# An encoder block on one core: four PSUM banks per tile in the first feed-forward product, a norm factor moved into the residual, SiLU as one function, and the last product's weights prepared in another stage

## The chip, the core and the metric

The kernel runs on one core of one Trainium2 chip. A core has five engines with a queue each: TensorE (PE, with its weight loads as PEld), VectorE (DVE), ScalarE (ACT), GpSimd (POOL) and SyncE (SP), which here issues all transfers. Each engine takes its instructions strictly in order; an instruction that waits for a semaphore holds up everything behind it on the same engine. The metric is the device time of one execution in microseconds, as the median of several runs. Times in this document are microseconds unless marked ns.

## The reference

Two sequences of 512 tokens with 1024 features go through one layer: a norm, a wide input projection, three branches (a state-space scan, a differential attention, a cross attention with a memory of 256 tokens), a gated merge, and a feed-forward part, then a final norm. The change touches the feed-forward part and the final norm:

```python
def _rmsnorm(x, g):
    y = xf * lax.rsqrt(jnp.mean(xf * xf, axis=-1, keepdims=True) + EPS)
    return (y * g.astype(jnp.float32)).astype(x.dtype)
...
    x = x + merged @ p['w_out'][l]
    xn2 = _rmsnorm(x, p['norm_ffn'][l])
    gate, up = jnp.split(xn2 @ p['w_ffn_in'][l], 2, axis=-1)
    return x + (jax.nn.silu(gate) * up) @ p['w_ffn_out'][l]
...
    return _rmsnorm(x, p['norm_final'])
```

The feed-forward width is 2816, which is 22 tiles of 128 columns. All arithmetic is fp32: each product is made of three TensorE products of a high and a low part (hh, hl, lh), so every fp32 weight or activation is first split, the high part by ACT (`L128`, or `L131` with a scale) and the low part by DVE (`L129`, or `L132` with a scale).

## The kernel before

The program is written as one function, `encoder`, and a scheduler fixes the order of each engine's queue when the program is built; where `PE.on` is true, TensorE keeps the order of the text. The stages, in time, are: memory and input projections with the state-space scan, cross attention, differential attention, merge, output projection (`out_tile`), first feed-forward product (called FFN-in here), second feed-forward product (FFN-out) and the final norm.

**Cross attention** (`L637` to `L685`) runs 32 steps of score, softmax, turn and output. Products from other stages are taken from a list (`queue`) and laid between the steps, so that TensorE has work while a softmax is made. Into the same steps goes `half_piece` (`L447`): one half of a *piece* of weights for FFN-out. There are 34 such pieces, made by the generator `prepare` (`L416`): two loads of `raw` from `w_fo` (`L402`, `L404`), four sums of 128x128 on POOL (`raw_sums`, `L411` to `L414`), a split into `hl` on ACT and DVE (`L131`, `L132`, with the scale 0.5), and a store to DRAM (`wD<-hl`, `L431`). FFN-out loads them later as `w<-wD`.

**FFN-in** (`L1069` to `L1098`) is a loop over 22 tiles. Both halves of a tile, gate and up, and both sequences together form a 2x2 block product, and it is made with seven products instead of eight (a Strassen-Winograd scheme). The seven have names: A11, S2, A12, S3, S1, A22 and S4. Each is 12 matmuls of 128x512 into a PSUM bank of its own, so a tile is 84 matmuls, and six banks rotate. The weights of a tile come as two loads (`wf<-in_w_fg` and `wf<-in_w_fu`, `L950` and `L951`); A11, A12 and A22 are splits of these, S1 to S4 are splits of four sums that POOL makes (`L965` to `L968`). `quadrants` (`L1049`) turns the seven banks into four quadrants with one ACT copy and seven DVE additions (`L1046`). Then, for each of the two sequences, the tile is finished so:

```python
            V.tensor_tensor(out=gf, in0=gf, in1=accs[s], op=ALU.mult)                                   # L1093
            last_t = S.activation(out=ac[:, cs], in_=gf, func=AF.Tanh, scale=0.5)                       # L1094
            PO.tensor_tensor(out=up, in0=up, in1=accs[s], op=ALU.mult)                                  # L1095
            V.scalar_tensor_tensor(out=ac[:, cs], in0=ac[:, cs], scalar=1.0, in1=gf, op0=ALU.add, op1=ALU.mult)  # L1096
            V.tensor_tensor(out=ac[:, cs], in0=ac[:, cs], in1=up, op=ALU.mult)                          # L1097
```

`accs[s]` holds the norm factor of each token; it is made while tile 0 is on TensorE (`L1087`, `L1088`). The result goes to DRAM (`aD`, `L1098`), twice too large (1 + tanh in place of a sigmoid), which the 0.5 in the splits of FFN-out's weights makes good.

**FFN-out** (`L1147` to `L1200`) takes the activations back from `aD`, sums and splits them (`act_pair`, `quad_split`), multiplies with the prepared and the freshly made weights, and adds to the residual `y`, which was stored to DRAM as `x1D` and is loaded again. The final norm (`final`, `L1214`) sums the squares of `y`, takes the root (`factor`, `L189`), spreads it over the partitions with TensorE transposes, and scales.

Of the kernel before, what the change touches and what calls it, by code (L numbers as in the profile page):

```python
# [19 lines left out]
P = 128  # L20
# [47 lines left out]
def encoder(ctx: ExitStack, tc: tile.TileContext, a, out):  # L68
# [112 lines left out]
    def rstd(acc, n, nt=4):  # L181


        ss = aux()
        for t in range(nt):
            PE.matmul(ss[:, t : t + 1], acc[:, t * P : (t + 1) * P], onec[:, 0:1], start=(t == 0), stop=(t == nt - 1))
        return factor(ss, n, nt)

    def factor(ss, n, nt=4, bias=epsc):  # L189

        rs = rp.tile([P, 4], F32, tag="rs", name="rs", bufs=4)
        S.activation(out=rs[:, :nt], in_=ss[:, :nt], func=AF.Sqrt, scale=1.0 / n, bias=bias)
        V.reciprocal(rs[:, :nt], rs[:, :nt])
        bc = aux()
        for t in range(nt):
            PE.transpose(bc[:, t * P : (t + 1) * P], rs[:, t : t + 1].broadcast_to([P, P]), ident)
        return rs, bc
# [218 lines left out]
    def prepare(es_):  # L416
        pq = es_.enter_context(tc.tile_pool(name="pq", bufs=1, side="right", reuse_waits="tile"))
        todo_, raws = [x_ for x_ in pieces if x_[2]], []

        def load():  # L420
            if len(raws) < len(todo_):
                raws.append(pq.tile([P, 4, P], F32, tag="raw", name="raw", bufs=4))
# [10 lines left out]
        for _ in range(3):  # L433
# [12 lines left out]

    def half_piece(behind_=()):  # L447
        with ExitStack() as es_:
            for i_ in behind_:
                es_.enter_context(tc.issue_after(i_.ins))  # L450
            return next(prep, None)
# [100 lines left out]

    pes = ExitStack()
    prep = prepare(pes)
    next(prep)


# [83 lines left out]
    for i in range(-AHEAD, len(steps) + 1):  # L641
# [41 lines left out]
    assert next(prep, None) is None  # L683
    pes.close()
# [320 lines left out]
    def product(ps, w, o, ks=range(4)):  # L1005
        wh, wl = w
        for k in ks:
            th, tl = ops[k]
            ws_ = slice(k * P, (k + 1) * P)
            PE.matmul(ps, wh[:, ws_], th[:, o], start=(k == 0), stop=False)  # L1010
            PE.matmul(ps, wh[:, ws_], tl[:, o], start=False, stop=False)
            PE.matmul(ps, wl[:, ws_], th[:, o], start=False, stop=(k == 3))
# [3 lines left out]
    def products(i, w):  # L1016
# [12 lines left out]
        elif i == KFF - 1:  # L1029
# [5 lines left out]
        else:  # L1035
            for nm, o in SEVEN:
                p_ = bank()
                product(p_, w[nm], o)
                yield p_
# [8 lines left out]

    def quadrants(ps, p0, other=("up", "gf")):  # L1049

        p1 = ap2.tile([P, L], F32, tag="p1", name="p1")
        S.copy(p1, p0)
# [8 lines left out]

    def act_pair(p, tag="ts"):
# [4 lines left out]
        return xa_, xb_, quad_sums(xa_, xb_, tag)  # L1067

    for i in range(KFF):  # L1069
        w = res0  # L1070
        if i > 0:
# [3 lines left out]
            next(wg)  # L1075
        if i == KFF - 3:
            open_tags(ses, side="right", ts=1)
# [5 lines left out]
        ps = products(i, w)  # L1083
        p0 = next(ps)
        if i == 0:
            for s in range(NS):
                _, bc = rstd(accs[s], DM)  # L1087
                S.copy(accs[s], bc)  # L1088
        gf0, gf1, up0, up1 = quadrants(ps, p0)
        ac = ap2.tile([P, NT], F32, tag="ac", name="ac")  # L1090
        for s, gf, up in ((0, gf0, up0), (1, gf1, up1)):
            cs = slice(s * L, (s + 1) * L)
            V.tensor_tensor(out=gf, in0=gf, in1=accs[s], op=ALU.mult)  # L1093
            last_t = S.activation(out=ac[:, cs], in_=gf, func=AF.Tanh, scale=0.5)  # L1094
            PO.tensor_tensor(out=up, in0=up, in1=accs[s], op=ALU.mult)  # L1095
            V.scalar_tensor_tensor(out=ac[:, cs], in0=ac[:, cs], scalar=1.0, in1=gf, op0=ALU.add, op1=ALU.mult)  # L1096
            V.tensor_tensor(out=ac[:, cs], in0=ac[:, cs], in1=up, op=ALU.mult)  # L1097
        nc.sync.dma_start(aD[i], ac)  # L1098

# [21 lines left out]
    def weights7(m, p, n):  # L1121
# [12 lines left out]
        if n < 7:  # L1134
            split(wa[:, :, 0], wa[:, :, 1], raw[:, 1:4], scale=0.5)
        if n == 0:
            raw_sums(raw)
            yield
            split(ws_[:, :, 0], ws_[:, :, 1], raw, scale=0.5)
# [12 lines left out]
    for v, (m, lo_, hi_) in enumerate(VISITS):  # L1152
# [34 lines left out]
        if v == 8:  # L1187
# [5 lines left out]
            for i in range(2 * NPAIR, KFF):  # L1193
# [3 lines left out]
                split(th, tl, ac, scale=0.5)  # L1197
# [4 lines left out]

    def ones(ss, sq, n, start=False, stop=False):

        for t in range(n // P):
            PE.matmul(ss[:, t : t + 1], sq[:, t * P : (t + 1) * P], onec[:, 0:1], start=(start and t == 0),
                      stop=(stop and t == n // P - 1))
# [6 lines left out]
    def final(ss, c0, n):  # L1214

        cs = slice(c0, c0 + n)
        _, bc = factor(ss, DM, n // P)
# [438 lines left out]
```

## Time and profile before

| | |
|---|---|
| median of 3 runs | 1651.76 us (1650.51 to 1655.25) |
| span of the profiled execution | 1652.8 us |
| PE / DVE / ACT / POOL busy in it | 97% / 70% / 39% / 33% |
| share of the chain of work that ended last | PE 69%, DVE 14%, DMA 6%, issue 5%, POOL 3%, ACT 2% |

The page gives the execution from its first to its last instruction (the span); it has no entry for time outside it, and the span stands 1.0 us above the median of the runs. "Busy" of a TensorE row includes waiting inside its pipeline, since ends of matmuls are modelled. In the windows view a line is one stretch of time: its length, then for PE, PEld, DVE, ACT and POOL the busy time with the number of instructions, the granted TensorE clock as a share of full speed, the DMA share and the GB/s. In the groups view a line is a set of equal instructions: engine, operation, out<-in, count, then busy time and the mean ns of one, then the idle time of the engine just before them and who ended it.

### The profile page before, as it was taken

To read this page: it belongs to the slowest core of one execution; us is meant where nothing else is said; L and a number is where in the kernel's file an instruction comes from. 1 tells how busy PE (TensorE), PEld (TensorE's weight loads), DVE (VectorE), ACT (ScalarE), POOL (GpSimd) and SP (SyncE) were. 2 spreads that over 40 slices of the span, in tenths; PEclk is the share of its full clock that TensorE was granted. 3 is DMA by queue.
4 is the path that set the end of the run, shared out by engine and by line. 5 is a ranking of instruction groups with operands and counts; after the bars stand their busy time and mean duration, and the time that the engine had idled before them with its cause. 6 is when DMAs were issued, how large, how long until landed. Compare 5 with 4: busy or idle time off the path is not lost.

```text
span 1652.8 us, 21658 instructions
## 1 busy us (share of the span) xinstructions
PE 1599.8 (97%) x7812; PEld 1316.8 (80%) x7812; DVE 1162.2 (70%) x1860; ACT 637.6 (39%) x1130; POOL 542.7 (33%) x444
## 2 busy tenths in 40 slices
PE   7999999899998999999999989999999999999997
PEld 5788788788887778877878878778888888778887
DVE  7957997155776666767365657888777777998655
ACT  6544323245554355565123442222223223242222
POOL 0001100001576222200243345565555553434352
PEclk9999999999999999999999999999999999999998
DMA  9354343737887111135453432322222222776522
GB/s 365 122 167 151 110 153 115 227 124 258 274 286 248 52 45 33 45 141 169 144 191 125 149 96 77 102 90 93 87 77 89 77 89 99 255 268 191 182 71 102
DMA packets 108202, 237.05 MB, mean 143 GB/s; under 512 B 13888, under 2 KB 50496, under 8 KB 108096
## 3 DMA queue, kind: packets, MB, share of 16 engines
q1 hardware_dynamic: 108096, 235.69, 42.8%
q8 instruction: 61, 1.00, 0.3%
q14 instruction: 45, 0.37, 0.1%
HBM read 166.73 MB, written 68.91 MB: 143 GB/s over the span
## 4 chain that ended last, share of the span: by engine, by line
PE 69%; DVE 14%; DMA 6%; issue 5%; POOL 3%; ACT 2%; SPq 1%; DVEq 0%; ACTq 0%; POOLq 0%
PE bkmm L61 60%; PE bktr L61 2%; DVE tl L129 2%; PE bksc L61 2%; DVE wl L129 2%; PE bkoo L61 1%; DMA raw<-in_w_fo 1%; PE bktr L64 1%; POOL up L1095 1%; DVE st L1527 1%; PE bktr L1509 1%; POOL mg L745 1%; DMA yt<-bD 1%; DMA fb<-aD 1%; DMA aD<-ac 1%
## 5 line engine op out<-in xcount | busy, mean ns | idle before, releaser
L61 PE MATMUL bkmm<-xh,wh 128*128 128x512 f32 x640 | 256.4, 401 | 3.9 <-DVE t L706 2.8
L61 PE MATMUL bkmm<-xh,wl 128*128 128x512 f32 x640 | 251.8, 394 | 2.3 <-DVE wl L129 2.3
L61 PE MATMUL bkmm<-xl,wh 128*128 128x512 f32 x640 | 251.5, 393 | 0.0
L61 PE MATMUL bkmm<-tl,wh 128*128 128x512 f32 (+1 forms) x621 | 242.8, 391 | 3.5 <-DVE tl L129 3.5
L61 PE MATMUL bkmm<-th,wl 128*128 128x512 f32 (+1 forms) x621 | 241.4, 390 | 3.5 <-DVE wl L129 3.5
L61 PE MATMUL bkmm<-th,wh 128*128 128x512 f32 (+1 forms) x621 | 243.0, 392 | 0.0
L128 ACT CAST wh<-wf 128x1024 fp32r<-128x1024 f32 (+1 forms) x133 | 117.8, 885 | 250.9 <-PE bkmm L61 229.2
L129 DVE TENSOR_TENSOR wl<-wf,wh 128x1024 fp32r<-128x1024 f32 (+1 forms) x133 | 141.7, 1065 | 70.2 <-ACT wh L128 59.9
L61 PEld LDWEIGHTS bkmm<-xh,wh 128*128 128x128 f32 x640 | 120.9, 189 | 35.3 <-issue 7.9
L61 PE MATMUL bkmm<-th,w 128*128 128x512 f32 x432 | 142.2, 394 | 5.4 <-DVE w L132 2.2
L61 PEld LDWEIGHTS bkmm<-xh,wl 128*128 128x128 f32 x640 | 120.8, 189 | 29.9 <-DVE wl L129 3.1
L61 PEld LDWEIGHTS bkmm<-tl,wh 128*128 128x128 f32 x621 | 117.5, 189 | 28.9 <-DVE tl L129 4.6
L61 PEld LDWEIGHTS bkmm<-th,wl 128*128 128x128 f32 x621 | 116.8, 188 | 29.7 <-DVE wl L129 6.3
L61 PEld LDWEIGHTS bkmm<-xl,wh 128*128 128x128 f32 x640 | 121.0, 189 | 22.6 <-issue 0.4
L61 PEld LDWEIGHTS bkmm<-th,wh 128*128 128x128 f32 x621 | 117.5, 189 | 25.2 <-ACT wh L128 1.2
L1095 POOL TENSOR_TENSOR up<-up,acc 128x512 f32<-128x512 f32 x44 | 84.5, 1941 | 125.8 <-DVE up L1046 125.8
L61 PEld LDWEIGHTS bkmm<-th,w 128*128 128x128 f32 x432 | 81.4, 189 | 27.0 <-DVE up L1046 4.0
L411 POOL TENSOR_TENSOR raw<-raw 128x128 f32<-128x128 f32 x34 | 20.7, 607 | 243.5 <-DMA wf<-in_w_in 198.6
L745 POOL TENSOR_TENSOR mg<-mg,gl 128x1024 f32<-128x1024 f32 x16 | 43.9, 2744 | 139.2 <-DVE gl L741 139.2
L504 ACT ACTIVATE e<-bksc,nb 128x512 f32<-128x512 f32 (+1 forms) x96 | 58.8, 615 | 71.3 <-DVE nb L499 50.3
L128 ACT CAST wh<-ws 128x1024 fp32r<-128x1024 f32 x44 | 46.1, 1051 | 102.8 <-PE bkmm L61 72.9
L61 PE MATMUL bkmm<-tl,w 128*128 128x512 f32 x216 | 84.6, 392 | 0.0
(634 smaller groups left out, 3569.3 us busy)
## 6 DMA issues: line engine op xcount, KB each, us to landing
wf<-in_w_in SPq DMA_DIRECT2D x40, 512.0 KB, 4.0
wD<-hl SPq DMA_DIRECT2D x34, 512.0 KB, 3.6
w<-wD SPq DMA_DIRECT2D x34, 512.0 KB, 3.8
gD<-gt SPq DMA_DIRECT2D x24, 512.0 KB, 3.0
gl<-gD SPq DMA_DIRECT2D x24, 512.0 KB, 3.4
wf<-in_w_fg SPq DMA_DIRECT2D x22, 512.0 KB, 3.5
wf<-in_w_fu SPq DMA_DIRECT2D x22, 512.0 KB, 3.5
aD<-ac SPq DMA_DIRECT2D x22, 512.0 KB, 2.6
```

The costliest lines, as they stand in the source:

```text
L61: return self.put(self.eng.matmul(*args, **kw))
L64: return self.put(self.eng.transpose(*args, **kw))
L128: h = S.copy(hi, src)
L129: l_ = V.tensor_tensor(out=lo, in0=src, in1=hi.bitcast(F32), op=ALU.subtract)
L411: PO.tensor_tensor(out=a22, in0=a21, in1=a22, op=ALU.add)
L504: last_x = S.activation(out=e, in_=sc, func=AF.Exp, bias=nb, scale=scale, accum_out=sm)
L745: PO.tensor_tensor(out=mg[m], in0=mg[m], in1=gt, op=ALU.add)
L1095: PO.tensor_tensor(out=up, in0=up, in1=accs[s], op=ALU.mult)
L1509: PE.matmul(ps[:, g * P : (g + 1) * P], w_[:, gg * P : (gg + 1) * P], u_[:, 8 * o + gg, :], start=True, stop=True)
L1527: V.tensor_tensor(out=sv[:, :, :, i], in0=p_, in1=q_, op=ALU.add)
```

## The change

Four things are changed, all in or for the feed-forward part.

1. `half_piece` and its calls leave cross attention. The same `prepare` is opened at tile 1 of FFN-in, and two halves are made after each of the tiles 1 to 18. `raw` has three buffers in place of four, `hl` two, and the splits have no scale.
2. `four_banks` makes the tiles 1 to 20. Three of the seven products add onto a bank that already holds another: A12 onto A11's after the ACT copy of it, S3 onto S2's after u2 was read, S4 onto S1's after c22 was read. Four banks and five additions are left; the first quadrant stays in its bank, and the factor is applied as it is read.
3. The up half is not scaled by the norm factor any more (`L1095` goes). Instead the residual is divided by the factor: `residual` loads `x1D`, multiplies by the root on POOL and stores it again, for eight tiles of features, after the tiles 2 to 9 in the text; the final norm, which takes a common scale of each token out, gets its epsilon scaled by the root's square (`qeps`).
4. Tanh and the two-operand step `L1096` become one `Silu` on ACT, and the 0.5 is gone from all splits.

```diff
-            hl = pq.tile([P, k, 2, P], F32R, tag=f"hl{k}", name="hl", bufs=k // 2)
-            split(hl[:, :, 0], hl[:, :, 1], w_, scale=0.5)
+            hl = pq.tile([P, 4, 2, P], F32R, tag="hl", name="hl", bufs=2)[:, :k]
+            split(hl[:, :, 0], hl[:, :, 1], w_)
...
-    pes = ExitStack()
-    prep = prepare(pes)
-    next(prep)
...
-        half_piece(last_e)
-        if i == -AHEAD:
-            half_piece(last_e)
...
+    def four_banks(w):
+        ba, bb, bc_ = (bank() for _ in range(3))
+        product(ba, w["A11"], 0)
+        p1 = kept_copy("p1", ba)
+        product(bb, w["S2"], 4)
+        u2 = summed("u2", bb, p1)
+        product(bc_, w["S1"], 3)
+        product(ba, w["A12"], 1, more=True)
+        product(bb, w["S3"], 5, more=True)
+        u3 = summed("u3", bb, p1)
+        c22 = summed("up", bc_, u3, 2)
+        bd = bank()
+        product(bd, w["A22"], 6)
+        c21 = summed("up", bd, u3, 2)
+        product(bc_, w["S4"], 2, more=True)
+        return ba, summed("gf", bc_, u2, 2), c21, c22
...
+    def residual(m):
+        t_ = slot("ld", name="xq")
+        nc.sync.dma_start(t_, x1D[m])
+        for s in range(NS):
+            cs = slice(s * L, (s + 1) * L)
+            PO.tensor_tensor(out=t_[:, cs], in0=t_[:, cs], in1=roots[s], op=ALU.mult)
+        nc.sync.dma_start(x1D[m], t_)
...
+        if i == 1:
+            prep = prepare(pes)
+            next(prep)
         if i == KFF - 3:
+            assert next(prep, None) is None
+            pes.close()
...
         if i == 0:
             for s in range(NS):
-                _, bc = rstd(accs[s], DM)
-                S.copy(accs[s], bc)
...
+                S.activation(out=rs, in_=ss[:, :4], func=AF.Sqrt, scale=1.0 / DM, bias=epsc)
+                rt = rp.tile([P, 4], F32, tag="ss", name="rt", bufs=3)
+                V.reciprocal(rt, rs)
+                S.copy(accs[s], spread(rt))
+                roots.append(rp.tile([P, L], F32, tag="nsq", name="root", bufs=2))
+                S.copy(roots[s], spread(rs))
+                V.scalar_tensor_tensor(out=rt, in0=rs, scalar=EPS * DM, in1=rs, op0=ALU.mult, op1=ALU.mult)
+                qeps.append(rt)
-        gf0, gf1, up0, up1 = quadrants(ps, p0)
+        gf0, gf1, up0, up1 = quadrants(ps, p0) if i in (0, KFF - 1) else four_banks(w)
...
-            V.tensor_tensor(out=gf, in0=gf, in1=accs[s], op=ALU.mult)
-            last_t = S.activation(out=ac[:, cs], in_=gf, func=AF.Tanh, scale=0.5)
-            PO.tensor_tensor(out=up, in0=up, in1=accs[s], op=ALU.mult)
-            V.scalar_tensor_tensor(out=ac[:, cs], in0=ac[:, cs], scalar=1.0, in1=gf, op0=ALU.add, op1=ALU.mult)
+            g_ = gf if s or i in (0, KFF - 1) else ap2.tile([P, L], F32, tag="gf", name="gf", bufs=2)
+            V.tensor_tensor(out=g_, in0=gf, in1=accs[s], op=ALU.mult)
+            S.activation(out=ac[:, cs], in_=g_, func=AF.Silu)
             V.tensor_tensor(out=ac[:, cs], in0=ac[:, cs], in1=up, op=ALU.mult)
         nc.sync.dma_start(aD[i], ac)
+        if 0 < i < KFF - 3:
+            for _ in range(2):
+                next(prep, None)
+        if 1 < i < 2 + KD:
+            residual(i - 2)
...
-        _, bc = factor(ss, DM, n // P)
+        nt, t0 = n // P, c0 % L // P
+        rs = rp.tile([P, 4], F32, tag="rs", name="rq", bufs=4)
+        V.tensor_tensor(out=rs[:, :nt], in0=ss[:, :nt], in1=qeps[c0 // L][:, t0 : t0 + nt], op=ALU.add)
+        _, bc = factor(rs, DM, nt, bias=0.0)
```

More of the change, by code (lines that the diff above doesn't have):

```diff
@@ L179, in new_acc, with ones @@
         return rp.tile([P, L], F32, tag="acc", name="acc", bufs=2)
[L181 to L187, printed above, removed]
+    def ones(ss, sq, n, start=False, stop=False):
+        for t in range(n // P):
+            PE.matmul(ss[:, t : t + 1], sq[:, t * P : (t + 1) * P], onec[:, 0:1], start=(start and t == 0),
+                      stop=(stop and t == n // P - 1))
     def factor(ss, n, nt=4, bias=epsc):
@@ L421, in load @@
             if len(raws) < len(todo_):
-                raws.append(pq.tile([P, 4, P], F32, tag="raw", name="raw", bufs=4))
+                raws.append(pq.tile([P, 4, P], F32, tag="raw", name="raw", bufs=3))
                 with queued():
@@ L1003, in encoder, with product @@
     aD = [drp.tile([P, NT], F32, name=f"aD{i}") for i in range(KFF)]
-    def product(ps, w, o, ks=range(4)):
+    def product(ps, w, o, ks=range(4), more=False):
         wh, wl = w
@@ L1047, in summed, with kept_copy @@
         return t_
+    def kept_copy(tag, p_):
+        t_ = ap2.tile([P, L], F32, tag=tag, name=tag)
+        S.copy(t_, p_)
+        return t_
     def quadrants(ps, p0, other=("up", "gf")):
-        p1 = ap2.tile([P, L], F32, tag="p1", name="p1")
-        S.copy(p1, p0)
+        p1 = kept_copy("p1", p0)
         u2 = summed("u2", next(ps), p1)
```

46 lines of the change are left out of this document (19 added, 27 removed).

## The prediction

> **What bounds the kernel now.** I read the page first, then the windows, then the chain and the waits of the stages that the change touches. The page and the windows (length, PE, PEld, DVE, ACT, POOL, granted clock, DMA share, GB/s):
>
> ```profile
> span 1652.8 us, 21658 instructions
> ...
> PE 1599.8 (97%) x7812; PEld 1316.8 (80%) x7812; DVE 1162.2 (70%) x1860; ACT 637.6 (39%) x1130; POOL 542.7 (33%) x444
> ```
> ```profile
> 471.00:475.00 4.00, 1.44 (x6) 0.65 (x5) 3.24 (x11) 2.53 (x8) 3.61 (x7) 1.00 0.60 201
> 521.00:529.00 8.00, 3.40 (x14) 2.05 (x13) 5.35 (x9) 3.85 (x7) 4.79 (x7) 0.88 0.81 293
> 527.50:534.00 6.50, 5.29 (x13) 4.13 (x14) 2.99 (x7) 0.63 (x1) 2.55 (x2) 0.50 0.46 185
> 984.40:998.40 14.00, 9.40 (x25) 6.03 (x25) 12.11 (x13) 8.77 (x12) 4.48 (x4) 0.63 0.00 0
> 1100.00:1390.00 290.00, 290.00 (x1281) 240.14 (x1280) 229.11 (x265) 86.52 (x108) 157.66 (x93) 1.00 0.25 85
> 1390.00:1450.00 60.00, 56.07 (x241) 44.58 (x240) 54.32 (x64) 22.04 (x30) 22.14 (x14) 1.00 0.68 227
> ```
>
> From 1100 to 1390, the body of FFN-in, PE has no gap: 290.00 over 1281 matmuls is 0.2264 each, 19.0 for the 84 of a tile. The change leaves those 84, so nothing can be won there: DVE's 229.11 of 290 (15.0 per tile) and POOL's 157.66 (10.3) lie beside PE. Gains are left only where PE waits: at both ends of the pieces' work in cross attention (two upper rows and the half clock behind them), at FFN-in's start, and in the DVE-bound stretch after 1390 (54.32 of 60). The chain and PE's waits from 415 to 560 say who holds it in cross attention:
>
> ```profile
> 465.65 6.50 DMA raw<-in_w_fo
> ...
> 528.71 24.54 PE bkmm L61 x96
> ...
> 1095.66 290.92 PE bkmm L61 x1282
> ...
> 1387.97 3.91 POOL up L1095 x2
> ```
> ```profile
> PE bkoo L61 <- ACT xpTh L128: 2.8, 2, 1.8
> PE bkmm L61 <- DVE t L706: 2.8, 1, 2.8
> PE bkoo L61 <- DVE xpTl L129: 1.6, 2, 0.8
> ```
>
> The load of a raw piece (6.50) stands on the chain, because ACT waits in order for it and PE waits for ACT.
>
> **Part 1, the pieces leave cross attention.** PE's order there does not change in the built program; only ACT, DVE, POOL and SP lose instructions. The three waits are 7.2. Behind ACT's and DVE's last `hl` the true dependencies stay: the last turn still needs its split and the next product's bank its evacuation. I keep 1.6 (the smallest of the three rows), so 5.6 go. Behind that wait 96 matmuls took 24.54; at 0.2264 they need 21.7, so the half clock (0.50 in the third window) cost 2.8, and goes if a wait of 1.6 does not bring it on. Sum: -8.4. Bounds: -10.0 (nothing stays) and -4 (only the ACT wait and half of the rest go). PE's next late item is then that evacuation.
>
> By the Trainium skill, "TensorE: Matmul & The Clock Gate", section "Part 1: The HAM clock gate", the clock halves after an idle window of about 3.4 us and returns after a busy one; the 0.50 agrees, and by that rule a wait of 1.6 costs no half clock.
>
> **Part 2, the pieces in FFN-in.** What one tile gains and loses, from the groups of 1100 to 1390, POOL's groups over the whole run, and the `hl` instructions (ns: min, median, max):
>
> ```profile
> L129 DVE TENSOR_TENSOR wl<-ws,wh 128x1024 fp32r<-128x1024 f32 x31 | 37.7, 1216 | 0.0
> L1096 DVE SCALAR_TENSOR_TENSOR ac<-ac,gf 128x512 f32<-128x512 f32 x31 | 37.6, 1214 | 0.0
> L1097 DVE TENSOR_TENSOR ac<-ac,up 128x512 f32<-128x512 f32 x30 | 35.4, 1179 | 18.2 <-POOL up L1095 17.7
> L1046 DVE TENSOR_TENSOR gf<-bkmm,p 128x512 f32<-128x512 f32 x31 | 21.3, 686 | 14.9 <-PE bkmm L61 14.9
> ```
> ```profile
> L1095 POOL TENSOR_TENSOR up<-up,acc 128x512 f32<-128x512 f32 x44 | 84.5, 1941 | 125.8 <-DVE up L1046 125.8
> ...
> L965 POOL TENSOR_TENSOR ws<-wf 128x512 f32<-128x512 f32 x22 | 39.7, 1804 | 58.5 <-DMA wf<-in_w_fu 46.4 <-DVE wl L129 9.5 <-ACT p L1052 2.6
> ...
> L966 POOL TENSOR_TENSOR ws<-ws,wf 128x512 f32<-128x512 f32 x22 | 35.3, 1602 | 1.4
> L967 POOL TENSOR_TENSOR ws<-wf,ws 128x512 f32<-128x512 f32 x22 | 29.6, 1348 | 0.2
> ...
> L412 POOL TENSOR_TENSOR raw<-raw 128x128 f32<-128x128 f32 x34 | 21.3, 626 | 2.7
> ```
> ```profile
> L131 ACT ACTIVATE hl<-raw x36: 514/632/651, 414.5 to 525.9; 128x512 fp32r<-128x512 f32 x34, 128x384 fp32r<-128x384 f32 x2
> L132 DVE SCALAR_TENSOR_TENSOR hl<-raw,hl x36: 548/692/984, 416.1 to 526.6; 128x512 fp32r<-128x512 f32 x34, 128x384 fp32r<-128x384 f32 x2
> ```
>
> DVE: two additions go (2 x 0.69), the two `L1096` go (2 x 1.21), two `hl` come (2 x 0.69): 15.0 - 2.4 = 12.6. POOL: two `L1095` go (3.9), eight sums of 128x128 come (8 x 0.6 = 4.8): 10.3 + 0.9 = 11.2. ACT gains 1.3 on 5.7 (86.52 over 15.2 tiles). `Silu` is in no row here; it should lie between no change from Tanh and twice its time (two ACT operations of some 0.6 more a tile at the end), and ACT has 12 free. All engines are below 19.0, so load alone costs nothing; order could.
>
> Transfers: two halves are four loads and two stores more on SP, 1.5 MB by the sizes in the code beside the 1.5 MB of a tile's `wf` and `aD`, so some 170 GB/s in place of 85, where 293 were reached from 521 to 529. On SP the stores wait for DVE's `hl`, and the next tile's `wf` loads stand behind them.
>
> I followed the queues of the built program through one tile, t counted from its first matmul. On DVE one 128x512 operation follows the other after 0.6 and a 128x1024 split takes 1.1, less than their durations:
>
> ```profile
> 1229.57 0.69 DVE L1093 TENSOR_TENSOR gf<-gf,acc 128x512 f32<-128x512 f32 x1
> 1230.18 1.22 DVE L129 TENSOR_TENSOR wl<-wf,wh 128x1024 fp32r<-128x1024 f32 x1
> 1231.32 0.68 DVE L1096 SCALAR_TENSOR_TENSOR ac<-ac,gf 128x512 f32<-128x512 f32 x1
> ```
>
> The bank waits, new with the four banks, are met: S3 comes 45 matmuls (10.2) after S2, A12 26 matmuls (5.9) after A11, and the previous tile's S4, now moved behind this tile's A11 and S2, leaves 26 matmuls (5.9) for u3 and c22 (1.4). DVE's addition that waits for this S4 (done at 8.6, with the pipeline at 9.1) has the whole tile's work queued behind it: two multiplications, u2, a split, two `hl`, a multiplication, a split, a multiplication and the low part of the next tile's A11. That is eight of 0.6 and three of 1.1, 8.2 in all, so it is done at 17.3 (the two `hl` counted at 0.7); if POOL slows all three multiplications between SBUF tiles to the 1.7 or 1.8 of the row at 1223.62 below, at 20.6. PE wants it 12 matmuls into the next tile, at 19.0 + 2.7 = 21.7. I take the middle, 19.0: PE stays fed, with some 2.5 to spare.
>
> The tightest thing is a round over four queues. SP can load the next `wf` only when DVE has split the old one; then POOL sums, then `hl`, then DVE splits again:
>
> ```profile
> 1219.40 0.33 SPq L951 DMA_DIRECT2D wf<-in_w_fu  x1
> ```
> ```profile
> 1223.00 1.85 POOL L965 TENSOR_TENSOR ws<-wf 128x512 f32<-128x512 f32 x1 [2.48 <-DMA wf<-in_w_fu]
> ```
> ```profile
> 1223.62 1.78 DVE L1096 SCALAR_TENSOR_TENSOR ac<-ac,gf 128x512 f32<-128x512 f32 x1
> ```
>
> Load to sum 3.6 (1219.40 to 1223.00); POOL 1.8 + 1.6 + seven of 0.6 = 7.6; first `hl` on ACT 0.6; then on DVE two `hl` 1.3, a multiplication slowed by POOL 1.7, a split 1.1, a multiplication 0.6, splits 1.1 and 0.7; hops 0.3. Sum 18.6, against a tile of 19.0. It just fits; I take 0, with the other side as the first rival.
>
> **Part 3, FFN-in's start.** The scheduler does not spread the eight residuals over tiles 2 to 9: in the built order their 16 POOL multiplications stand ahead of tile 2's weight sums, eight of them ahead of tile 1's. What was there before:
>
> ```profile
> 984.48 0.59 ACT L1088 COPY acc<-bktr 128x512 f32<-128x512 f32 x1
> ...
> 1007.00 1.06 ACT L128 CAST wh<-ws 128x1024 fp32r<-128x1024 f32 x1 [12.54 <-PE bkmm L61]
> ...
> 1020.18 1.05 ACT L128 CAST wh<-ws 128x1024 fp32r<-128x1024 f32 x1 [4.62 <-PE bkmm L61]
> ```
> ```profile
> 994.33 2.19 POOL L965 TENSOR_TENSOR ws<-wf 128x512 f32<-128x512 f32 x1 [9.52 <-DVE wl L129]
> ...
> 1008.59 3.52 POOL L1095 TENSOR_TENSOR up<-up,acc 128x512 f32<-128x512 f32 x2 [7.76 <-DVE up L1046]
> ```
> ```profile
> 975.00:1025.60 50.60, 43.48 (x170) 33.00 (x170) 8.43 (x13) 1.17 (x2) 0.90 0.18 58
> ```
>
> The first root is there at about 986.7 (after 984.48: a copy, four transposes, a second copy). From there POOL has, up to the sum S2 of tile 2, 16 multiplications, nine sums of 128x128 and seven weight sums. At 1.6 each (between 1.3, `L967`, and 1.95, `L1095`), 0.6 and 1.65 that is 25.6 + 5.4 + 11.6 = 42.6: 1029.3, and ACT's split is done at 1030.5. Tile 1's sum S2 is done after eight, five and three of them, 20.8, at 1007.5, which is when ACT came to it before (1007.00, after PE had freed the buffer), so it costs nothing. PE reaches tile 2's S2 after two tiles' worth of matmuls: the last row counts 170 of FFN-in by 1025.6; with 1.0 for the extra copy (0.6) that now stands ahead of the split for PE's next operand, and for eight more transposes that mostly fall into PE's gaps of 984 to 998 (9.40 busy of 14.00), 1026.6. So PE waits about 4, and with 1.0 of half clock behind it (the fourth window shows 0.63 after such waits) part 3 costs 1.0 + 4 + 1.0 = +6. Bounds: at 1.3 POOL is 4.8 earlier and only +1 stays; at 1.95 it is 5.6 later, +12. Residual loads and stores wait for POOL on SP's queue, and tile 3's `wf` behind them; it is wanted 6 later than it comes.
>
> **Part 4, the end.** `L1095` leaves the chain at 1387.97 (3.91), and DVE loses two `L1096` in the last tile, in a stretch where PE loses 60 - 56.07 = 3.9 to a full DVE. I take -1, between 0 and -3. In the final norm one small DVE addition enters the last chain; the nearest row is a reciprocal of the same size:
>
> ```profile
> 1645.33 0.17 DVE L193 RECIPROCAL rs<-rs 128x2 f32<-128x2 f32 x1 [1.91 <-ACT rs L192]
> ```
>
> +0.2 with its hop.
>
> **Sum.** -8.4 + 0 + 6 - 1 + 0.2 = -3.2 on the span of 1652.8: 1649.6. The span stands 1.0 above the median, so the forecast is 1649.
>
> **Rivals.** (a) *Slower: the round of part 2 decides.* If it takes longer than 19.0, each tile lasts as long as the round, once the 2.5 to spare are used up. It needs 0.4 more than I counted: one more multiplication slowed to 1.7 or 1.8 as at 1223.62 is 1.1, a 7.6 on POOL that becomes 8.5 is 0.9. For it: `L1095` took 1.94 where `L967` took 1.35, so POOL slows when DVE is busy. Against it: my path already has one slowed multiplication, and 1231.32 shows 0.68 with POOL idle. At 0.7 over, 18 tiles give 12.6 - 2.5 = 10.1: 1659, from 1652 to 1672. (b) *Every split is slowed as `L1096` was.* Then three splits and two `hl` cost 1.1 more in the round: 18.6 + 5.5 is 5.1 over, 18 tiles give 92 - 2.5 = 89: 1738. Against it: `wl<-ws` kept 1.216 over 31, some of them beside POOL. The Trainium skill, "GPSIMD Engine Reference", section "Specifications", says that POOL's SBUF interfaces contend with DVE instructions that have two SBUF inputs, which the splits are; the 1.216 speaks against it for them. (c) *No wait at tile 2,* since DVE is less busy at 986 to 1025 and POOL runs at 1.3: 1644. (d) *The waits in cross attention do not go,* because the order of the text holds PE there too: -8.4 becomes about -2, 1655. Against it: two of the three waits name splits that queue behind `hl`.
>
> **Chances.** Forecast 0.47 (own range 1643 to 1656: faster 0.22, same 0.21, slower 0.04), (a) 0.29 (slower 0.27, same 0.02), (b) 0.02 slower, (c) 0.15 (faster 0.13, same 0.02), (d) 0.07 (same 0.04, slower 0.03). About 0.3%, 5.0, is what a measurement of this kernel can tell from no change: faster is below 1646.8, slower above 1656.7. Sums: faster 0.35, same 0.29, slower 0.36. The range that leaves 0.2 out takes in the forecast's own, (c)'s better part and (a) to 1666: 1640 to 1666.
>
> **What would show it.** In the changed profile: from 425 to 530 no PE wait over 2 and no 0.50 behind it; FFN-in at 19.0 per tile (rival a: an even period above it, with PE waiting for DVE's `wl`); one PE wait near tile 2 for ACT's `wh<-ws`, with POOL full since the roots; `L1127` sometimes 0.7, sometimes 1.7. The prediction is wrong if FFN-in grows by more than 12, or if cross attention gains less than 4.

## The result and the profile after

The changed kernel takes 1669.28 us (median of 4 runs, 1665.6 to 1670.75), the kernel before 1651.13 in the same comparison: the ratio is 1.0100, with a 95% interval from 1.0082 to 1.0119. It is slower, 20 us above the forecast and outside the range. The profiled execution took 1670.45, with a span of 1668.7; the span of before was 1652.8, so 15.9 is to be explained. The page of the changed kernel: span, TensorE and the other engines, and the chain by engine.

```profile
span 1668.7 us, 21552 instructions
...
PE 1607.5 (96%) x7820; PEld 1318.1 (79%) x7820; DVE 1115.6 (67%) x1781; ACT 634.1 (38%) x1132; POOL 480.7 (29%) x416
...
PE 68%; DVE 11%; issue 7%; DMA 6%; POOL 5%; ACT 2%; SPq 1%; DVEq 0%; POOLq 0%; ACTq 0%
```

DVE lost 46.6 of busy time and POOL 62, and the kernel is longer: the share of busy time told nothing. What grew on the chain is POOL (3% to 5%) and "issue" (5% to 7%). Stretches of the changed kernel in the windows view (two of cross attention, one of FFN-in's start, one of its body), and PE's waits from 415 to 560 and from 1044 to 1349:

```profile
465.00:472.00 7.00, 7.00 (x37) 5.82 (x36) 4.03 (x13) 3.03 (x9) 0.00 (x0) 1.00 0.00 0
515.00:523.00 8.00, 6.23 (x29) 4.62 (x28) 3.04 (x5) 1.75 (x4) 0.57 (x1) 1.00 0.13 32
1012.00:1025.00 13.00, 8.75 (x31) 6.46 (x29) 8.07 (x7) 3.12 (x5) 13.00 (x12) 0.87 0.76 269
1100.00:1300.00 200.00, 195.27 (x843) 156.71 (x842) 133.78 (x149) 62.06 (x90) 106.58 (x125) 1.00 0.44 158
```
```profile
PE bkoo L61 <- ACT xpTh L128: 1.0, 1, 1.0
PE bkoo L61 <- DVE xpTl L129: 0.8, 1, 0.8
```
```profile
PE bkmm L61 <- ACT wh L128: 6.0, 7, 1.9
PE bkmm L61 <- DVE wl L129: 2.4, 8, 0.4
PE bkmm L61 <- DVE u L1026: 2.1, 1, 2.1
```

Cross attention did what was forecast: PE is full from 465 to 472, of the 7.2 of waits 1.8 are left, and the clock behind them is 1.00. The body of FFN-in did not: from 1100 to 1300 PE made 843 matmuls where 200 us hold 884 at 0.2264. Many small waits, most for a weight split, make it up; the view of the waits leaves out the smallest.

For the comparison by stage, the start of every 84th matmul of FFN-in is taken as the start of a tile, so that tile 0 begins with FFN-in's first matmul:

| | before | after | difference |
|---|---|---|---|
| up to FFN-in's first matmul | 975.06 | 966.20 | -8.9 |
| tiles 0 to 2 | 69.55 | 77.85 | +8.3 |
| tiles 3 to 17 | 290.11 | 304.73 | +14.6 |
| tiles 18 to 20 | 57.12 | 58.92 | +1.8 |
| from tile 21 to the last matmul | 254.04 | 254.08 | 0.0 |

(In the expectations below the third row is called tiles 3 to 18, from the first matmul of the one to that of the other. The last row takes 249 to 254 in the kernels that follow, and 260 in e12; part 4 below comes back to it.)

Fifteen tiles of 84 matmuls need 285.6; the kernel before lost 4.5 in its tiles 3 to 5, the changed one loses something in every tile: from tile 6 to tile 16 each takes 19.5 to 20.6, 19.9 in the mean.

One tile of the changed kernel, from the timeline of each queue (start, duration, engine, line, out<-in; in brackets the idle time before it and who ended it). First the round that the prediction had counted at 18.6, in order of time:

```profile
1206.77 0.33 SPq L936 DMA_DIRECT2D wf<-in_w_fu  x1
...
1211.52 1.29 POOL L950 TENSOR_TENSOR ws<-wf 128x512 f32<-128x512 f32 x1 [9.41 <-DMA wf<-in_w_fu]
...
1218.46 1.14 ACT L128 CAST hl<-raw 128x512 fp32r<-128x512 f32 x2 [5.04 <-POOL raw L416]
...
1219.11 3.25 DVE L129 TENSOR_TENSOR hl<-raw,hl 128x512 fp32r<-128x512 f32 x2 [2.26 <-ACT hl L128]
1222.29 0.68 DVE L1127 TENSOR_TENSOR ac<-ac,up 128x512 f32<-128x512 f32 x1
1222.89 1.21 DVE L129 TENSOR_TENSOR wl<-ws,wh 128x1024 fp32r<-128x1024 f32 x1
1224.03 0.68 DVE L1127 TENSOR_TENSOR ac<-ac,up 128x512 f32<-128x512 f32 x1
1224.63 1.81 DVE L129 TENSOR_TENSOR wl<-wf,wh 128x1024 fp32r<-128x1024 f32 x2
...
1225.90 0.33 SPq L935 DMA_DIRECT2D wf<-in_w_fg  x1
1226.47 0.33 SPq L936 DMA_DIRECT2D wf<-in_w_fu  x1
```

From one load of the up half to the next, 1206.77 to 1226.47, is 19.70, and the matmuls of this tile take as long (the ten such steps around this one are 19.5 to 20.4). Every link waits for the one above it: POOL was idle for 9.41 until the load was there, ACT for 5.04 until POOL's raw sums were, DVE for 2.26 until ACT's copy was. All `hl` splits of the run (ns: min, median, max), and the median landing of the loads:

```profile
L129 DVE TENSOR_TENSOR hl<-raw,hl x36: 680/1539/1792, 986.8 to 1320.2; 128x512 fp32r<-128x512 f32 x34, 128x384 fp32r<-128x384 f32 x2
```
```profile
wf<-in_w_fg SPq DMA_DIRECT2D x22, 512.0 KB, 3.8
wf<-in_w_fu SPq DMA_DIRECT2D x22, 512.0 KB, 4.5
```

In the kernel before the median `hl` took 692 ns, and both loads landed after 3.5:

```profile
wf<-in_w_fg SPq DMA_DIRECT2D x22, 512.0 KB, 3.5
wf<-in_w_fu SPq DMA_DIRECT2D x22, 512.0 KB, 3.5
```

### The profile page after: what moved, and what is told of

The parts are those of the page before. It is cut to its first block, busy times and chain, and to the rows that moved or that the text cites. A ratio compares the mean times of both kernels' runs of the same rounds, so it can differ in the third digit from the quotient of the medians.

```text
span 1668.7 us, 21552 instructions
## 1 busy us (share of the span) xinstructions
PE 1607.5 (96%) x7820; PEld 1318.1 (79%) x7820; DVE 1115.6 (67%) x1781; ACT 634.1 (38%) x1132; POOL 480.7 (29%) x416
## 4 chain that ended last, share of the span: by engine, by line
PE 68%; DVE 11%; issue 7%; DMA 6%; POOL 5%; ACT 2%; SPq 1%; DVEq 0%; POOLq 0%; ACTq 0%
PE bkmm L61 57%; DVE wl L129 3%; PE bktr L61 2%; PE bksc L61 2%; DMA wf<-in_w_fu 2%; PE bkoo L61 2%; PE bktr L64 2%; DVE tl L129 2%; POOL xq L1082 1%; PE bktr L1541 1%; DMA c_n<-cD 1%; POOL mg L730 1%; DMA yt<-bD 1%; DVE hl L129 1%; POOL raw L414 1%
## 5 line engine op out<-in xcount | busy, mean ns | idle before, releaser
L61 PE MATMUL bkmm<-th,wl 128*128 128x512 f32 (+1 forms) x621 | 237.1, 393 | 4.3 <-DVE wl L129 3.9
L692 POOL TENSOR_TENSOR t<-t,rs 128x512 f32<-128x512 f32 x16 | 24.7, 1547 | 455.5 <-DVE t L691 421.5
L61 PEld LDWEIGHTS bkmm<-xl,wh 128*128 128x128 f32 x640 | 120.4, 188 | 22.4 <-issue 0.4
L129 DVE TENSOR_TENSOR hl<-raw,hl 128x512 fp32r<-128x512 f32 (+1 forms) x36 | 54.0, 1530 | 37.8 <-ACT hl L128 37.8
```

The lines of the kernel that those rows point to most:

```text
L61: return self.put(self.eng.matmul(*args, **kw))
L129: l_ = V.tensor_tensor(out=lo, in0=src, in1=hi.bitcast(F32), op=ALU.subtract)
L692: PO.tensor_tensor(out=t2, in0=t2, in1=rope[1], op=ALU.mult)
```

## The experiments

My theory after the result: the round (load, POOL's sums, raw sums, `hl`, the splits that free the load's buffer, next load) sets the tile. Rivals: the new bank waits of four banks; the pieces' traffic; the form of `hl`, which is a plain subtraction now and was a multiply-subtract before; an engine that is simply full.

**e1: the same work, `hl` at another place on DVE.**

```diff
-            for _ in range(2):
-                next(prep, None)
+            with tc.issue_after(last_sum.ins):      # DVE: behind this tile's gf
+                for _ in range(2):
+                    next(prep, None)
```

> The changed kernel with both hl splits of a tile placed on DVE behind that tile's last sum gf, instead of between the two wl<-ws splits; the same instructions, the same work. Round theory: in the changed kernel DVE takes u2, wl<-ws, hl, hl, ac, wl<-ws, ac, wl<-wf, wl<-wf in that order; hl waits for the POOL sums that wait for the wf load, and the next wf load waits for wl<-wf, so load 4.75 + POOL 7.3 + hl and splits 7.9 close a round of 19.5 to 19.7 us a tile. With hl behind gf the round loses the raw sums (2.5) and the two hl (3.25): tiles 3 to 18 go back from 304.7 to 286 to 290, and the kernel from 1669.3 to 1654 (1651 to 1658). Rival, four banks: the new waits of S4, S3 and u3 on four banks set the 19.7; then nothing changes, 1669 (1666 to 1672). Rival, traffic: the pieces' 2 MB of loads and stores a tile slow the wf load by 1.1 us; then half stays, 1662.

Measured: 1648.64 against 1651.62, ratio 0.9982 (0.9970 to 0.9994). Twenty us come back from one edit that removes nothing.

```profile
1100.00:1300.00 200.00, 200.00 (x884) 165.58 (x884) 141.69 (x159) 72.47 (x97) 120.72 (x123) 1.00 0.49 164
```
```profile
L129 DVE TENSOR_TENSOR wl<-ws,wh 128x1024 fp32r<-128x1024 f32 x29 | 51.0, 1758 | 2.3 <-ACT wh L128 2.3
L129 DVE TENSOR_TENSOR hl<-raw,hl 128x512 fp32r<-128x512 f32 x29 | 19.5, 714 | 0.1
```

PE is full again, with DVE and POOL busier in the same 200 us (141.69 and 120.72) than in the changed kernel (133.78 and 106.58). Four banks and traffic fall as causes: both are still there, and tiles 3 to 17 take 287.2. The slowing by POOL did not go either; it moved to `wl<-ws` (1758 ns), where it costs nothing. 287.2 lies inside the 286 to 290 that were expected, and the kernel is 2 below its range.

**e2: the pieces back in cross attention** (`prepare` is opened there again, with `half_piece` and four `raw` buffers, as in the kernel before; the other three changes stay).

> The changed kernel with the pieces' preparation put back into cross attention (four banks, the root in the residual and the Silu stay). Round theory: FFN-in has no raw sums, no hl and no traffic of theirs; tiles 3 to 18 take 286 to 290 (changed kernel 304.7), cross attention takes back its 8.9 us of waits: 1669.3 - 15 + 8.9 = 1663 (1659 to 1666). Rival, four banks: tiles 3 to 18 stay at 304 and cross attention costs 8.9 more: 1678.

Measured: 1652.43, ratio 1.0012 (0.9999 to 1.0025), 10 below what I expected. Tiles 3 to 17 take 285.6, the bare matmuls, so the pieces are what made the round too long. Of the 10, tiles 3 to 17 gave 4 more than expected and FFN-in's start fell by 3.5, to 74.3; cross attention took back 5.8 of its 8.9, for FFN-in starts at 971.99. And one rival falls for good, the pieces' traffic: no piece is loaded in FFN-in here, yet the load is as late as in the changed kernel.

```profile
1214.07 0.33 SPq L950 DMA_DIRECT2D wf<-in_w_fg  x1
1214.64 0.33 SPq L951 DMA_DIRECT2D wf<-in_w_fu  x1
```
```profile
wf<-in_w_fu SPq DMA_DIRECT2D x22, 512.0 KB, 4.5
```

Here, as in the changed kernel, SP issues both loads of a tile 0.57 apart; in the kernel before they were issued 7 us apart, with no other transfer issued between them:

```profile
1212.42 0.33 SPq L950 DMA_DIRECT2D wf<-in_w_fg  x1
1219.40 0.33 SPq L951 DMA_DIRECT2D wf<-in_w_fu  x1
```

**e3: `hl` in the form of before.**

```diff
-            split(hl[:, :, 0], hl[:, :, 1], w_)
+            split(hl[:, :, 0], hl[:, :, 1], w_, scale=1.0)
```

> The changed kernel with the hl splits written as multiply by 1.0 and subtract (scalar_tensor_tensor, the form of the kernel before) instead of a plain subtraction; the order on DVE is unchanged. If the form is what took hl from 0.69 us (before) to 1.54 us: hl is back at 0.7 to 0.9, the round is shorter by 1.7, tiles 3 to 18 fall to about 288 to 293 and the kernel to 1656 (1653 to 1661). If it is POOL working beside it (its 128x512 sums of the weights' own): hl stays at 1.3 to 1.8 and the kernel at 1669 (1666 to 1672).

Measured: 1666.68, ratio 1.0101 (1.0086 to 1.0116); tiles 3 to 17 take 303.1. The form is not it:

```profile
L132 DVE SCALAR_TENSOR_TENSOR hl<-raw,hl x36: 676/1535/1789, 988.8 to 1322.2; 128x512 fp32r<-128x512 f32 x34, 128x384 fp32r<-128x384 f32 x2
```

**e4: seven banks in the tiles 1 to 20** (`products` and `quadrants` as before; pieces in FFN-in, residual and `Silu` stay).

> The changed kernel with seven banks a tile in tiles 1 to 20, as before (order A11, S2, A12, S3, S1, A22, S4); pieces in FFN-in, the residual's root and the Silu stay. Here DVE's order has wl<-wf ahead of hl, and the next wf load stands on SP's queue ahead of only one of the hl stores. Round theory: the round does not contain hl; tiles 3 to 18 take 286 to 291 and the kernel 1655 (1652 to 1660). Four-banks theory: the same number, for the other reason; the first kernel of this call tells the two apart. If DVE's two more sums a tile or POOL beside DVE are what costs: 1666 or more.

Measured: 1652.38, ratio 1.0009 (0.9993 to 1.0025). The median load of the up half lands after 3.5 here, with the pieces' traffic, which confirms e2's reading, and the median `hl` takes 693 ns. Tiles 3 to 17 take 295.7, more than I expected: one tile (17, 23.5) and smaller losses in the others, whose cause is not shown.

**e13: the round broken on POOL instead.** The raw sums go behind the last of the tile's four weight sums; no edge is put on DVE.

```diff
-        PO.tensor_tensor(out=s34[:, :H], in0=a1[:, :H], in1=a2[:, :H], op=ALU.subtract)
+        last_q = PO.tensor_tensor(out=s34[:, :H], in0=a1[:, :H], in1=a2[:, :H], op=ALU.subtract)
...
-            for _ in range(2):
-                next(prep, None)
+            with tc.issue_after(last_q.ins):        # POOL: behind the weight sums
+                for _ in range(2):
+                    next(prep, None)
```

> The changed kernel with the pieces' raw sums on POOL behind the last of the tile's four weight sums; nothing else is tied (the residual still stands in tiles 0 to 2), and the scheduler then puts hl on DVE behind the two up sums and ahead of gf. Round theory: the wf load's round holds only the four weight sums (4.8), not the raw sums and hl; tiles 3 to 18 take 286 to 289 and the kernel is where e1 is, 1649 (1646 to 1653). If raw sums and hl had to be kept away from the tile's bank releases on DVE too (gf now waits behind hl): tiles of 19.3 to 19.8, 1655 to 1660.

Measured: 1652.68, ratio 1.0001 (0.9989 to 1.0012). Tiles 3 to 17 take 285.6, tile 18 takes 21.7 (19.04 in the changed kernel), and FFN-in's start keeps its 77.9.

```profile
1100.00:1300.00 200.00, 200.00 (x884) 165.62 (x883) 139.39 (x157) 68.78 (x94) 120.87 (x126) 1.00 0.51 171
```

The scheduler, which was free to, also put `hl` elsewhere on DVE, so e1 and e13 show two edits that open the round, and not which of the two links alone would do.

**e5 to e9: the residual.** e5 is the changed kernel with each residual tile's load tied behind its own tile's `wf` loads, so that two POOL multiplications stand in each of the tiles 2 to 9:

```diff
-            residual(i - 2)
+            with queued():                          # SP: behind this tile's wf loads
+                residual(i - 2)
```

> The changed kernel with each residual tile's load queued on SP behind its own tile's wf loads, so that the 16 root mults on POOL no longer stand in tiles 0 to 2 but two a tile in tiles 2 to 9; hl stays where it is. Theory: from FFN-in's start to tile 3 the changed kernel takes 77.85 us (before 69.55) because tile 2's weight sums wait behind 16 mults; spread, 70 to 73 is left, and each of tiles 2 to 9 has two mults (2.4 us) more in the round wf load, POOL, hl, wl: up to 1 us more for each of the eight. Net -5 + 4: 1668 (1664 to 1673). Rival, the start is the root's own copies and transposes: 77 to 78 stays, and the tiles still lengthen: 1672. If the round theory is false the tiles don't lengthen: 1663.

Measured: 1680.74, ratio 1.0164 (1.0149 to 1.0180), 11 slower than the changed kernel where I expected no change; PE's waits from 1044 to 1200, and one of the pairs of multiplications between the raw sums:

```profile
PE bkmm L61 <- ACT wh L128: 15.7, 7, 3.6
```
```profile
1122.12 3.96 POOL L1082 TENSOR_TENSOR xq<-xq,root 128x512 f32<-128x512 f32 x2
```

I had priced two multiplications at 2.4 and up to 1 us a tile; they took 4.0 here, and tiles 3 to 17 grew by 16. It is the round again, with a dose: what is put between the load and `hl` lengthens the tile. The other half of the expectation failed too: the start was to fall to 70 to 73, and takes 76.8.

e6 has both edits, e1's and e5's.

> Both edits: hl behind gf (1648.6 by itself) and the residual tiles spread. Round theory: the round has some 8 us to spare once hl is out of it, so two POOL mults more a tile cost nothing, the tiles stay at 19.04, and FFN-in's start falls from 73.6 to 70 to 71: 1645 (1642 to 1648). Rival, POOL and DVE slow each other: every DVE operation of two SBUF inputs beside the mults takes about twice as long, the tiles of the spread grow by 0.5 each and the gain is gone: 1649.

Measured: 1649.72, ratio 0.9979 (0.9967 to 0.9991). The start fell to 68.6 as expected (tiles 1 and 2 at 19.04), but tiles 3 to 17 grew from 287.2 to 295.7. e9 puts the two multiplications behind the weight sums as well:

```diff
-            with queued():
+            with queued(), tc.issue_after(last_q.ins):
                 residual(i - 2)
```

> The changed kernel with hl behind gf, and each residual tile's load behind its tile's wf loads and its two POOL mults behind the last of that tile's four weight sums. With the residuals spread but ahead of two of the four sums the start was 68.6 instead of 73.6, and six tiles grew by 5.1 together. If those 5.1 came from the sums waiting behind the mults: the start stays at 68.6 to 69.5, the tiles fall back to 19.04, 1644 (1641 to 1647). If they came from POOL slowing DVE's operations beside it, or from the xq traffic: the tiles keep their 5, 1649.

Measured: 1644.28, ratio 0.9954 (0.9937 to 0.9971), as expected: start 68.9, tiles 3 to 17 289.4 (not quite back at the bare 285.6). This is faster than both kernels, with all four changes in it and only the order altered. e14 moves the residual on to tiles 10 to 17 and gives tile 20 seven banks:

> e9 (1644.3: hl behind gf, residual's mults behind the weight sums) with seven banks in tile 20 and the residuals in tiles 10 to 17. If the four banks cost the 2.6 us at the step into tile 21, this comes back; if the mults cost 0.4 a tile only where POOL or DVE were still behind from the start, tiles 3 to 18 fall from 289.4 to 287: 1640 (1638 to 1644). If the 2.6 belong to tile 21's own loads and the mults cost the same later: 1644.

Measured: 1644.84, ratio 0.9947 (0.9931 to 0.9962): no gain. The multiplications cost 0.2 to 1.0 a tile where they are, and tiles 3 to 17 rise to 292.6. The step from tile 20 into tile 21 is 21.2. Every kernel with four banks shows a long step there (20.8 to 21.7); the kernel before, e4, e7 and e11, with seven banks, have 19.04 (e12, with seven too, has 22.4, but its tiles 3 to 17 take 21.8 each in the mean). Part 4 below names the wait; e14 has another one in its place.

**e7, e8, e11, e12, e10: parts alone.** e7 is the kernel before with only the pieces moved:

> The kernel before with only the pieces moved into FFN-in (seven banks, Tanh, up's mult on POOL, no residual). Here DVE takes wl<-wf ahead of the first hl of a tile. Round theory: the round does not hold both hl, cross attention gives 8.9 and the tiles stay at 19.04 to 19.3: 1643 (1640 to 1648). Rival, DVE full: hl (1.4 to 3.2 us a tile) comes on DVE's 15.0 us beside 15 us of POOL, slowed operations make it 19 or more and each tile waits: 1655 (1650 to 1665).

Measured: 1689.26, ratio 1.0218 (1.0200 to 1.0236): far worse than either theory. e12 adds e1's edge to it:

> The kernel before with the pieces in FFN-in (1689.3 so) and hl behind the tile's last sum gf. If its 21.7 us a tile were the same round through raw sums and hl (and the wf loads that stand on SP's queue behind hl's stores): tiles 19.04 to 19.6, 1648 (1643 to 1655). If they come from up's mult on POOL standing behind raw sums (ac waits for it, 15.3 us of the window) and from DVE's operations slowed beside a fuller POOL: 1675 to 1690.

Measured: 1694.08, ratio 1.0262 (1.0243 to 1.0282). Here e1's cure does nothing (tiles 3 to 17 take 331.0 in e7 and 326.9 in e12), and the round theory as I had it misses. DVE's waits from 1050 to 1320, e7 first, then e12:

```profile
DVE hl L132 <- ACT hl L131: 51.3, 13, 4.0
DVE ac L1096 <- POOL up L1094: 14.2, 12, 1.2
```
```profile
DVE ac L1095 <- ACT ac L1093: 34.2, 14, 2.8
DVE ac L1096 <- POOL up L1094: 14.6, 12, 1.6
```

With `hl` out of the way DVE still waits 49 us elsewhere, and in both kernels 14 to 15 of it for POOL's `up`, the multiplication that the residual's root removes in the changed kernel. e4 has the same banks and the same pieces, and besides them the residual and `Silu`, and takes 1652.4 in place of 1689.3: the pieces need these two changes, taken together, to fit. Which wait of e12 would have to go is open.

e8 is the kernel before with only the four banks, e11 the residual and `Silu` with seven banks and the pieces in cross attention:

> The kernel before with only the four banks a tile (Tanh and up's mult on POOL stay, the pieces stay in cross attention). Here DVE's order has ac, wl<-wf, ac, wl<-wf, with ac waiting for Tanh and for POOL's mult. Round theory: load to POOL 4.7, sums 4.8, wl<-ws and the two ac chains some 7, wl<-wf 2: about 18.5, just inside 19.04: 1651 (1649 to 1655). If the four banks' own waits cost: each tile grows by 0.3 to 0.6 and the time is 1657 to 1662. If two DVE sums fewer a tile were worth something where DVE is not the bound: 1648.

> Seven banks, pieces in cross attention, only the residual's root and the Silu of the change. POOL loses up's mult, DVE one multiply-add; 16 mults stand on POOL in tiles 0 to 2. Expected: start 69.6 + 4 to 6, tiles 19.04, end unchanged: 1655 (1652 to 1658). If the mults don't stand in the way of tile 2: 1650.

e8: 1657.37, ratio 1.0024 (1.0010 to 1.0038), above the 1649 to 1655 that I expected; tiles 3 to 17 as before (290.0), the step into tile 21 is 21.4, 2.4 longer. Two DVE additions fewer bring nothing where DVE isn't the bound. e11: 1645.33, ratio 0.9966 (0.9954 to 0.9977), 10 better than I expected: its tiles 3 to 17 take 285.6 instead of 290.1, and FFN-in's start 70.6, though the 16 multiplications stand in tiles 0 to 2 as in the changed kernel. By themselves they cost little. e10 is e9 with seven banks in all tiles:

> The same with seven banks a tile in tiles 1 to 20. With seven banks the last step into tile 21 takes 19.04 (four banks: 20.9 to 21.6), and two sums more stand on DVE a tile. If the order of hl and of the residual was the only cost of the seven-bank version (1652.4; its start took 75.4, its tiles 3 to 18 295.7): start 70, tiles 287 to 289, 1642 (1639 to 1646). If DVE's two sums more close another round (wl<-wf stands between gf and u3): tiles of 19.3, 1648.

Measured: 1647.69, ratio 0.9980 (0.9968 to 0.9992), nearer to the rival's 1648 than to mine; the reason is open.

## Why the prediction was wrong, point by point

**Part 1 (-8.4): right.** Measured -8.9. Of the 7.2 of waits 1.8 are left, where 1.6 was kept: one for the high and one for the low part of the same split. The wait for the bank's evacuation (2.8), which the prediction called PE's next late item, is gone whole, and the half clock with it. It is not this execution alone: FFN-in starts at 964.0 to 968.2 in the changed kernel, e1, e3 to e7, e9 and e12 to e14, which have the pieces moved, and at 972.0 to 975.3 in the kernel before, e2, e8 and e11, which have not.

**Part 2 (0): wrong, and this is the step that failed:** "Sum 18.6, against a tile of 19.0. It just fits; I take 0, with the other side as the first rival." The links were the right ones in the right order, and the round did decide; its terms, measured in the tile above, were:

| term | predicted | measured |
|---|---|---|
| load to sum | 3.6 | 4.75 |
| POOL, up to ACT's `hl` | 7.6 | 6.94 |
| first `hl` on ACT | 0.6 | 0.65 |
| two `hl` on DVE | 1.3 | 3.18 |
| `ac` | 1.7 | 0.60 |
| `wl<-ws` | 1.1 | 1.14 |
| `ac` | 0.6 | 0.60 |
| splits of `wf`, then both loads | 1.8 | 1.84 |
| hops | 0.3 | in the rows above |
| sum | 18.6 | 19.70 |

Two terms were too small. The load's 3.6 was read from a trace in which the two loads of a tile are 7 us apart; the changed queue issues them together (e2, e4). And the slowing by POOL was counted once, at 1.1, on the `ac`, where the trace of before had shown it; in the new order POOL's last two weight sums run under the two `hl`, and both are slowed, by 1.9 together, while the `ac` no longer meets POOL and takes 0.60. POOL was overestimated by 0.7. A sum that misses its limit by 0.4, from terms that can each err by one, was no ground for 0.47 against 0.29.

**Rival (a) was what happened.** It named the round, a period over 19.0 and PE waiting for weight splits. Its overrun of 0.7 is that of the tile above (19.70), but the mean of tiles 3 to 17 is 20.3. It gave +10.1 for FFN-in's tiles and 1659; tiles 3 to 17 gave +14.6, the start 2.3 more than part 3, and the end 1.8 in place of -1, which leads to within 1.2 of the 1669.3, inside its 1652 to 1672.

**Part 3 (+6): right in the cause, wrong in the wait; that the size is near is luck.** Measured +8.3: tile 0 +1.6, tile 1 +5.6, tile 2 +1.1. The forecast had PE wait 4 us for tile 2's S2, whose sum stands behind POOL's multiplications. That split ended at 1023.2 (counted: 1030.5 in the time of before, 1021.6 here), and PE waited 0.8 for its low part. The larger wait, 3.7 and the half clock after it, came earlier and by another way, from POOL to ACT to DVE to PE:

```profile
1005.99 7.46 POOL L1082 TENSOR_TENSOR xq<-xq,root 128x512 f32<-128x512 f32 x4
1013.41 0.46 POOL L416 TENSOR_TENSOR raw<-raw 128x128 f32<-128x128 f32 x1
```
```profile
1013.91 1.03 ACT L128 CAST hl<-raw 128x512 fp32r<-128x512 f32 x2 [5.36 <-POOL raw L416]
```
```profile
1014.56 2.64 DVE L129 TENSOR_TENSOR hl<-raw,hl 128x512 fp32r<-128x512 f32 x2 [2.25 <-ACT hl L128]
1017.12 0.68 DVE L1026 TENSOR_TENSOR u<-bkmm,p 128x512 f32<-128x512 f32 x1
```
```profile
1017.85 0.80 PE L61 MATMUL bkmm<-th,wh 128*128 128x512 f32 x1 [3.73 <-DVE u L1026]
```

Four multiplications of the residual hold up the last raw sum, that holds up both `hl`, and behind them on DVE stands the addition that frees a bank. The prediction had only looked at what the multiplications do to the weight sums, not at the raw sums between them. Where the raw sums are gone, the forecast wait is there: e2 has four banks and the 16 multiplications but no raw sums in FFN-in, and its PE waits 3.1 at the first matmul of tile 2, for the split of S2:

```profile
1024.81 0.50 PE L61 MATMUL bkmm<-th,wh 128*128 128x512 f32 x1 [3.10 <-ACT wh L128]
```

Its start takes 74.3, 4.8 over before; with seven banks (e11) the same multiplications cost 1.1. So this cost, too, is one of order: e1 takes 4.2 of it away, e6 and e9 all, with tiles 1 and 2 at 19.04.

**Part 4 (-0.8): the sign of the sum was wrong.** The step into tile 21 is 1.8 longer, and the trace names the wait:

```profile
1404.84 0.50 PE L61 MATMUL bkmm<-th,wh 128*128 128x512 f32 x1 [1.51 <-DVE up L1026]
```

This is the 73rd of tile 20's 84 matmuls, the first of its last product, S4, which adds onto the bank that the addition `up` has to read first. In the tiles before, S4 stands behind the next tile's A11 and S2, as the prediction says; tile 20 has no four-bank tile behind it, and only A22 is left in between. The same matmul waits 1.51 in e1, e2, e3, e5, e6, e9 and e13 and 2.1 in e8; e14, with seven banks in tile 20, does not have this wait but one of 1.0 for ACT's `wh` and one of 0.5 for `u`. That the last four-bank tile has no cover for its S4 stood nowhere in the prediction.

The -1 itself does not show in the last row of the table (254.0 and 254.1), but the granted clock there differs. From tile 21 on it is 0.50 for two stretches of 3.4 us in this execution of the changed kernel (from 1451.3 and from 1495.7), and for one in that of before and of e8 (254.0). Of the other kernels with the residual's root and `Silu`, e2, e6, e9, e11, e13 and e14 have one such stretch and take 249.6 to 251.7; e1, e3, e4 and e5 have none and take 249.2 to 251.1. So at the same number of half-clock stretches the end is some 2 to 4 shorter, which is more than was forecast, and in this one execution the second stretch hid it. What brought that stretch on is not shown.

**Rival (b)** said that splits are slowed as the multiplication was, and was put at 0.02 on the mean of `wl<-ws` (1.216) in the kernel before. That mean was true of one order of the queues only: it is 1758 in e1, and the median `hl` takes twice its time in the changed kernel (1539 against 692). The price in (b), every split, is still too high, because most splits of a tile don't meet POOL: in the tile above both `wl` rows after the `hl` have their own times. **Rivals (c) and (d)** did not occur.

## What the runs showed of the hardware

In the rows below a DVE operation of two SBUF operands and a POOL operation do not share time: one stands until the other is done. POOL's last two weight sums of the tile above:

```profile
1218.82 1.28 POOL L952 TENSOR_TENSOR ws<-wf,ws 128x512 f32<-128x512 f32 x1
1220.07 1.75 POOL L953 TENSOR_TENSOR ws<-wf 128x512 f32<-128x512 f32 x1
```

The first ends at 1220.10; the first `hl`, begun inside it at 1219.11, takes 1.54 and ends 0.55 after it. POOL's second sum takes 1.75 instead of 1.28 and ends at 1221.82; the second `hl` ends 0.55 after that. Which operations suffer is seen in two groups of the changed kernel, 1060 to 1330: the same multiplication with its operand in SBUF and in PSUM, one right behind the other on DVE while POOL works.

```profile
L1125 DVE TENSOR_TENSOR gf<-gf,acc 128x512 f32<-128x512 f32 x13 | 13.7, 1053 | 0.0
...
L1125 DVE TENSOR_TENSOR gf<-bkmm,acc 128x512 f32<-128x512 f32 x13 | 8.8, 679 | 0.0
```

The Trainium skill says this in "SBUF — State Buffer", section "SBUF: two separate sides": when a DVE operation has two SBUF inputs and a GpSimd operation reads SBUF, whichever starts first has the shared port pair for the whole instruction, and the other fully blocks. The rows agree: 0.68 with a PSUM operand, and with two SBUF operands the own time plus what is left of POOL's. So the mean of such a group is a fact of the order of two queues and does not carry over to another order.

The second fact is on transfers. Two loads of 512 KB issued 0.57 apart land after 3.8 and 4.5 (medians), against 3.4 to 3.5 when they are 7 to 8 us apart. The 0.5 MB of loads and 1 MB of stores that the pieces add to a tile made no difference to either (the changed kernel and e4 with them, e2 and the kernel before without). What is issued in the same microsecond does: in e8 the 512 KB store of `aD` stands between the two loads, 1.15 apart there, and they land after 4.2 and 5.5.

## What to carry to other kernels

When work is moved under a stage that has engines to spare, write down the round of queues that one iteration closes, and treat a sum within one slowed instruction of the limit as a coin toss, not as a fit; a price read from the old order (a load alone on the queues, an operation that didn't meet POOL) is not a price in the new one. If the round comes out too long, look for an edge that takes the new work out of it before giving the change up: here a few such edges, with nothing removed, turned +1.0% into -0.5%. Parts of a change need not add: the pieces alone cost 2.2%, the residual and `Silu` alone gave 0.3%, and the first needs the second.
